# Attention output, norm and first feed-forward products of layer 2, rearranged by token block

## The chip, the cores and the metric

The kernel runs on one core of a Trainium2 chip. The metric is the device time of one execution in microseconds (us); the time before is the median of three runs. PE is the matrix engine (TensorE), PEld its weight loads, DVE the vector engine, ACT the scalar (activation) engine, POOL GpSimd, and SP the engine whose queue issues most weight loads.

## The reference

A trunk of two layers over 256 latent tokens and 256 context tokens of width 1024. Layer 1 mixes tokens with an mLSTM, layer 2 with multi-head latent attention; each is followed by a gated feed-forward with a short convolution over time. The change lies in layer 2, where only the latent tokens are still needed:

```python
x = _layer_norm(ALPHA * x + ml[2] * yl, ln_g[i, 0], ln_b[i, 0])      # yl = attention output @ w_out
f = _conv_ffn(_modulate(x, ml[3], ml[4]), ffn_w_in[i], ffn_conv_w[i], ffn_conv_b[i], ffn_w_out[i])
x = _layer_norm(ALPHA * x + ml[5] * f, ln_g[i, 1], ln_b[i, 1])

def _conv_ffn(h, w_in, conv_w, conv_b, w_out):
    gate, up = jnp.split(h @ w_in, 2, axis=-1)                       # FFN_DIM = 2816 columns each
    return (jax.nn.silu(_dwconv(gate, conv_w, conv_b)) * up) @ w_out
```

## The kernel before, in words

**Numbers in two parts.** Every product is made in a rounded format (`F32R`): an operand is split into a high part (a rounded copy, made by ACT) and a low part (the rest, `tensor_sub` on DVE). A product is then three matmuls: high by high, high by low, low by high (`mm3`, lines 395, 396 and 397).

**Weights.** `Stream` brings the weights in, in one fixed order, as tiles of 128 x 1024. `_load` issues the transfer on SP's queue into a raw tile; `_split` lets ACT make the high part (L334) and DVE the low part (L337), and then frees the raw tile. Around the change the raw tiles have nine places, reused in a ring, and a load is issued only when a place of its kind is free. Tiles marked wide (the last seven of `aout`, and of `fin1` those of p = 0 and 1) are split into two tiles `wu` of the pool `u` (31 tiles); the others into one of three tiles `w`. `use` hands over the next weight tile and splits ahead, up to eight tiles and up to `st.limit`; `pump(n)` splits up to tile n. In the order, the eight tiles `aout` come first, then the tiles `fin1` (p, j) for p = 0 to 21, j = 0 for the gate and 1 for the up projection, then `fout1`.

**The stage.** The 256 latent tokens are two blocks (t = 0, 1) of 128. `outmm` multiplies the attention output by `aout`; its last seven tiles are taken block by block. Block 0 has two column pieces of 512, block 1 has one of 512 and two of 256 (`acc4(True)`), so that less is left to do after the last. `ln_rows` then works through both blocks: gate times product, plus residual, `bn_stats` by piece, `bn_aggr`, square root on ACT (L1164), and normalization on DVE (L1187) and ACT (L1189). `ln_T4` transposes both blocks on PE (L1243, tiles `zT`, two column groups of both blocks to a PSUM bank), with five filler matmuls (`IDLE`, L1248) between the blocks, and makes from each of the eight transposed column groups k the feed-forward's input: scale and shift on ACT (L1255) or DVE (L1257), high part on ACT (L1258), low part on DVE (L1259), 256 tokens at a time, into the tiles `h1u`. `h1u` holds, for each k, 256 high columns and then 256 low ones.

**The feed-forward.** `ffn_in` runs over p and j; for p = 0 and 1 a product is 24 matmuls of 256 columns by `mm3`. From p = 2 on (L1374) the high weights multiply high and low activations in one matmul of 512 columns, the low weights the 256 high ones: 8 + 8 matmuls; the two halves are then added by a copy on ACT (L1378) and an addition on DVE (L1379), in a tile `fs`. The convolution, SiLU and gate follow for each p (`conv`, L674 to L681, L1385, L1393, L1394). `ln_x` applies the norm's gain and bias to the normalized rows (L1282, L1283) and stores them for the residual of the last step; it is advanced one step at each product (`tick`).

**What sets the order.** The program's instructions go through a scheduler which orders each engine's work by its own estimate of when operands are ready and by the order of the program. `keep_in_program_order` (`pin`) fixes an instruction behind the one traced before it on its engine; `issue_after(x)` puts what is traced in its block behind x on x's engine. On the chip each engine works its own list in order. [...]

Of the kernel before, what the change touches and what calls it, by code (L numbers as in the profile page):

```python
# [23 lines left out]
ALPHA = float((2 * DEPTH) ** 0.25)  # L24
# [7 lines left out]
CW = 1024  # L32

NB, NRAW, NU, NS = 3, 3, 31, 15

SUMS = 5

IDLE = 5

AHEAD = 8  # L40
QA, QB, QC = 2, 4, 6
PA, PB, PC = 0, 2, 4

VE = {1: (3, 0), 2: (3, 0), 3: (3, 0)}
# [209 lines left out]
class Stream:  # L254


    def __init__(self, k, ids, order, ws):
        self.k, self.ids, self.order, self.ws = k, ids, order, ws
        self.n = len(order)
        self.nl = self.ns = self.nu = 0  # L260
        self.live, self.kept = [], []
        self.limit = self.n
        self.raw, self.hl, self.tags = {}, {}, {}
        self.nsum = 0

        keys = [x[0] for x in order]
# [47 lines left out]
    def _split(self):  # L314
        k, j = self.k, self.ns
        key, wide = self.order[j]
        cols = self.ids[key][1]
        while self.nl <= j:
            self._load()
        self.nsum = max(self.nsum, j)  # L320
        while self.nsum < min(j + SUMS, self.n):
            while self.nl <= self.nsum:
                self._load()
            self._sum(self.nsum)
            self.nsum += 1
# [8 lines left out]
        k.nc.scalar.copy(h[:, :cols], src)  # L334
        if key[0] in ("vt2", "yt2"):
            k.nc.scalar.dma_start(k.t2d[key[0][0], key[1], key[2]][:, :cols], src)
        k.nc.vector.tensor_sub(l[:, :cols], src, h[:, :cols])  # L337
        self.hl[j] = (h, l)
        self.ns += 1
        while self._room():  # L340
            self._load()

    def use(self, key, hold=False):
        i = self.nu
# [21 lines left out]
class K:  # L366
# [863 lines left out]
                    yield  # L1230
            yield

    def ln_T4(self, zs, A, B, dst):


        nc, pin = self.nc, self.tc.keep_in_program_order
        w = self.st.hl[self.st.nu][0]
        pts = [self.ps("zT") for _ in range(4)]
        idle = self.ps("idle")
        for t in range(2):  # L1240
            for k in range(8):
                o = (k % 2) * 256 + t * 128
                i = nc.tensor.transpose(pts[k // 2][:, o:o + 128], zs[t][:, k * 128:(k + 1) * 128], self.ident)  # L1243
                if t and not k:
                    pin(i)
            if not t:
                for _ in range(IDLE):
                    pin(nc.tensor.matmul(idle, w[:, 0:128], w[:, 0:512], start=True, stop=True))  # L1248

        def one(k):  # L1250
            c = slice((k % 2) * 256, (k % 2 + 1) * 256)
            p, m = pts[k // 2][:, c], tmp[:, c]
            hi, lo = dst(k)
            if k // 2 % 2 == 0:
                nc.scalar.activation(m, p, AF.Identity, bias=B[:, k:k + 1], scale=A[:, k:k + 1])  # L1255
            else:
                nc.vector.tensor_scalar(m, p, A[:, k:k + 1], B[:, k:k + 1], op0=ALU.mult, op1=ALU.add)  # L1257
            i = nc.scalar.copy(hi, m)  # L1258
            nc.vector.tensor_sub(lo, m, hi)  # L1259
            return i.ins  # L1260

        tmp = self.s2("zm")
        first = one(0)
        for k in range(1, 8):
            if k % 2 == 0:
                tmp = self.s2("zm")
            with self.tc.issue_after(first):
                one(k)
            if k % 2:
                yield  # L1270

    def ln_x(self, ln, zs, dst):

# [73 lines left out]
    def ffn_in(self, l, hT, n, nt, pre=(), both=None):  # L1347

        nc, st = self.nc, self.st
        cw, cb = self.smc("fcw%d" % l), self.smc("fcb%d" % l)  # L1350
        key = "fin%d" % l
        acts = []
        pre = list(pre)
        for p in range(NF):
            pss = []
            for j in range(2):
                if pre:
                    w, ps = pre.pop(0)
                    self.ffn_half(ps, w, hT, 1)
                    if not pre:  # L1360
                        st.unhold()
                else:
                    w = st.use((key, p, j))
                    ps = self.ps("fin")
                    if both is None or p < 2:
                        for k in range(8):
                            c = slice(k * 128, (k + 1) * 128)
                            self.mm3(ps[:, :n], (w[0][:, c], w[1][:, c]), hT(k), k == 0, k == 7)
                    else:

                        mms = [(0, k) for k in range(7)] + [(1, k) for k in range(8)] + [(0, 7)]
                        for i, (x, k) in enumerate(mms):
                            c = slice(k * 128, (k + 1) * 128)
                            nc.tensor.matmul(ps[:, :n] if x else ps, w[x][:, c],  # L1374
                                             hT(k)[0] if x else both(k), start=i == 0, stop=i == 15)
                    if both is not None and p > 1:
                        t = self.s2("fs")
                        nc.scalar.copy(t[:, n:2 * n], ps[:, n:2 * n])  # L1378
                        nc.vector.tensor_tensor(t[:, :n], ps[:, :n], t[:, n:2 * n], op=ALU.add)  # L1379
                        ps = t  # L1380
# [474 lines left out]
def build(tc, off, a, out):  # L1855
    es = ExitStack()
    with es:
        k = K(tc, es, off, a)
        nc = k.nc
# [52 lines left out]
        def after0(pss, xr, gate, g, ln, l, c, dst, xdst):  # L1912
# [4 lines left out]
            yield from (k.ln_T4(zs, A, B, dst) if l else k.ln_T(zs, A, B, dst, g == 1))  # L1917
            if xdst is not None:
                k.late.append(k.ln_x(ln, zs, xdst))

# [38 lines left out]
        def norm1(g, zs, stats, first):  # L1959
# [6 lines left out]
            if g:  # L1966
# [24 lines left out]
        st.limit = fi + QA  # L1991
        k.outmm("aout", range(8 - TAIL["aout"], 8), o1, pl, 0, 8, 1, True)
        oT = None
        h1u = [k.u("h1") for _ in range(4)]
        h1 = lambda i: tuple(h1u[i // 2][:, i % 2, n * 256:(n + 1) * 256] for n in range(2))
        x3d = k.dr.tile([2, 128, D], F32, name="x3d")
        k.bg = [after0(pl, xr, gate, 1, 2, 1, 3, h1,
                       [x3d[0], x3d[1]])]
        k.tick(1)
        st.pump(fi + QB)  # L2000
        k.tick(1)
        st.pump(fi + QC)
        k.drain()
        st.limit = st.n
        k.take_late()
        acts = k.ffn_in(1, h1, 256, 1, both=lambda i: h1u[i // 2][:, i % 2])
        k.drain()
        h1 = h1u = None
        act1 = lambda i: (acts[i][:, 0], acts[i][:, 1])
# [27 lines left out]
```

## Time and profile before

| | |
|---|---|
| runs | 1359.81, 1359.42, 1362.17 us (median 1359.81) |
| the profiled execution | 1359.2 us; its span, first to last instruction, 1357.4 us |
| granted TensorE clock | 0.999 |
| PE busy | 1342.4 us, 99% of the span |
| DVE, ACT busy | 1056.4 us (78%), 711.9 us (52%) |
| attention output to feed-forward | about 1139 to 1176.5 us of the span |
| first products of layer 2's feed-forward (p = 0, 1) | 1164.9 to 1176.5 us |
| the later ones (p = 2 to 21) | 1176.5 to about 1288 us |

Times within the profile are counted from the start of the span. In a row of a timeline stand start, length, engine, line, operation, output and inputs, shapes, and in brackets the idle time before it with the instruction that ended it. A matmul's length is longer than its step: back-to-back matmuls overlap, and the distance of their starts is what they cost.

### The profile page before, as it was taken

The numbers are of one execution on the slowest core, as the hardware profiler recorded it, in microseconds if no ns is written. First come the engines' busy times: TensorE is split into PE (matmuls) and PEld (weight loads), VectorE is DVE, ScalarE is ACT, GpSimd is POOL, SyncE is SP. The second block draws the span as 40 slices with busy tenths as digits, with TensorE's granted clock in tenths as the row PEclk, the third lists the DMA queues.
The fourth block names the chain that finished last, engine by engine and source line by source line (L and its number), as shares of the span: only waits on it lengthen the run. The fifth ranks groups of instructions, "written<-read, shape, count | busy, mean of one in ns | idle before, by whom it ended". The sixth has DMA issues, their size and how long they took to land.

```text
span 1357.4 us, 18736 instructions
## 1 busy us (share of the span) xinstructions
PE 1342.4 (99%) x6663; PEld 1120.6 (83%) x6663; DVE 1056.4 (78%) x1731; ACT 711.9 (52%) x1236; POOL 122.1 (9%) x216
## 2 busy tenths in 40 slices
PE   9999999999999999999999999999999999999997
PEld 6777888888888888888898888888888888888886
DVE  4787756677688697897979878667898889888873
ACT  4764544445734545464644334334557767466660
POOL 0122000011101011030001000000001000000100
PEclk9999999999999999999999999999999999999999
DMA  9887848789676374785727877646997436366750
GB/s 368 315 271 269 294 162 245 235 289 304 215 250 194 98 246 142 239 297 190 232 92 250 295 234 236 213 148 215 309 279 220 140 102 223 104 192 188 256 194 31
DMA packets 92078, 297.73 MB, mean 219 GB/s; under 512 B 12073, under 2 KB 16425, under 8 KB 91985
## 3 DMA queue, kind: packets, MB, share of 16 engines
q1 hardware_dynamic: 62848, 218.65, 48.7%
q0 software_dynamic: 17472, 57.57, 13.6%
q10 hardware_dynamic: 11664, 20.32, 4.2%
q8 instruction: 52, 0.85, 0.3%
q14 instruction: 42, 0.34, 0.1%
HBM read 263.03 MB, written 33.46 MB: 218 GB/s over the span
## 4 chain that ended last, share of the span: by engine, by line
PE 93%; DMA 3%; DVE 2%; ACT 1%; issue 1%; ACTq 0%; SPq 0%; DVEq 0%
PE fin L1374 8%; PE y L396 6%; PE y L397 6%; PE y L395 6%; PE fin L395 6%; PE fin L396 6%; PE fin L397 6%; PE tok L395 6%; PE tok L396 6%; PE tok L397 6%; PE qk L395 4%; PE qk L397 4%; PE qk L396 4%; DMA adaw<-in_ada 2%; PE up L395 2%; PE up L397 1%
## 5 line engine op out<-in xcount | busy, mean ns | idle before, releaser
L337 DVE TENSOR_TENSOR w<-raw,w 128x1024 fp32r<-128x1024 f32 (+2 forms) x286 | 343.8, 1204 | 140.0 <-ACT w L334 139.2
L334 ACT CAST w<-raw 128x1024 fp32r<-128x1024 f32 (+2 forms) x286 | 297.2, 1039 | 290.8 <-PE tok L397 78.4
L500 DVE SCALAR_TENSOR_TENSOR junk<-ar,bc 128x1024 f32<-128x1024 f32 x128 | 156.2, 1220 | 4.0 <-ACT bc L542 1.4
L396 PE MATMUL fin<-h,w 128*128 128x512 f32 (+1 forms) x376 | 141.2, 376 | 0.0
L397 PE MATMUL fin<-h,w 128*128 128x512 f32 (+1 forms) x376 | 140.9, 375 | 0.0
L395 PE MATMUL fin<-h,w 128*128 128x512 f32 (+1 forms) x376 | 140.8, 376 | 0.1
L1374 PE MATMUL fin<-h,w 128*128 128x256 f32 (+1 forms) x640 | 111.9, 337 | 0.0
L1374 PEld LDWEIGHTS fin<-h,w 128*128 128x128 f32 x640 | 98.3, 190 | 13.4
L395 PE MATMUL qk<-xc,w 128*128 128x512 f32 x256 | 100.6, 393 | 0.0
L397 PE MATMUL qk<-xc,w 128*128 128x512 f32 x256 | 99.9, 390 | 0.0
L396 PE MATMUL qk<-xc,w 128*128 128x512 f32 x256 | 99.8, 390 | 0.0
L396 PEld LDWEIGHTS fin<-h,w 128*128 128x128 f32 x376 | 70.8, 188 | 12.9 <-DVE h L1228 0.2
L397 PEld LDWEIGHTS fin<-h,w 128*128 128x128 f32 x376 | 70.8, 188 | 12.9
L395 PEld LDWEIGHTS fin<-h,w 128*128 128x128 f32 x376 | 70.5, 188 | 13.1 <-ACT h L1227 0.3
L397 PEld LDWEIGHTS qk<-xc,w 128*128 128x128 f32 x256 | 48.1, 188 | 9.8
L396 PEld LDWEIGHTS qk<-xc,w 128*128 128x128 f32 x256 | 48.1, 188 | 9.7
L395 PEld LDWEIGHTS qk<-xc,w 128*128 128x128 f32 x256 | 48.1, 188 | 9.7
L395 PE MATMUL tok<-w,hT 128*128 128x512 f32 x128 | 49.9, 390 | 0.0
L397 PE MATMUL tok<-w,hT 128*128 128x512 f32 x128 | 49.8, 389 | 0.0
L396 PE MATMUL tok<-w,hT 128*128 128x512 f32 x128 | 49.8, 389 | 0.0
L681 ACT ACTIVATE fg<-fg 128x512 f32<-128x512 f32 (+1 forms) x44 | 23.2, 527 | 46.1 <-DVE fg L679 39.9
L337 DVE TENSOR_TENSOR wu<-raw,wu 128x1024 fp32r<-128x1024 f32 (+1 forms) x37 | 43.7, 1204 | 4.1 <-ACT wu L334 3.9
(470 smaller groups left out, 3142.3 us busy)
## 6 DMA issues: line engine op xcount, KB each, us to landing
raw<-in_ws SPq DMA_DIRECT2D x282, 512.0 KB, 4.6
ar<-in_adaT SPq DMA_DIRECT2D x80, 512.0 KB, 4.6
adaw<-in_ada SPq DMA_DIRECT2D x16, 512.0 KB, 8.0
t2d<-raw ACTq DMA_DIRECT2D x13, 512.0 KB, 4.8
raw<-t2d SPq DMA_DIRECT2D x13, 512.0 KB, 6.6
raw<-in_ws POOLq DMA_DIRECT2D x13, 512.0 KB, 7.9
zr<-fd ACTq DMA_DIRECT2D x33, 128.0 KB, 4.6
xmd<-xr POOLq DMA_DIRECT2D x16, 256.0 KB, 4.8
```

The costliest lines, as they stand in the source:

```text
L334: k.nc.scalar.copy(h[:, :cols], src)
L337: k.nc.vector.tensor_sub(l[:, :cols], src, h[:, :cols])
L395: mm(out, w[0], x[0], start=start, stop=False, skip_group_check=on)
L396: mm(out, w[0], x[1], start=False, stop=False, skip_group_check=on)
L397: mm(out, w[1], x[0], start=False, stop=stop, skip_group_check=on)
L500: nc.vector.scalar_tensor_tensor(o, w, 1.0, self.bc[j], op0=ALU.mult, op1=ALU.mult, accum_out=col[:, k, j:j + 1])
L681: nc.scalar.activation(tmp[:, :n], tmp[:, :n], AF.Silu)
L1374: nc.tensor.matmul(ps[:, :n] if x else ps, w[x][:, c], hT(k)[0] if x else both(k), start=i == 0, stop=i == 15)
```

## The change

`ln_T4` and the call of `after0` for layer 2 go; a new function `aout_fin` writes the stage out by token block.

- All `aout` tiles are split; then the four tiles `fin1` of p = 0 and 1 get their high parts only, and (2, 0) both. `Stream._split` leaves the low parts undone while `st.later` is a list; the raw tiles stay occupied until `low` is called.
- Block 0 is summed and normalized (on ACT alone) while PE multiplies block 1. Its eight transposes come between the second and the third column piece of block 1, into two banks.
- For block 0, column groups 0 to 5 are scaled, shifted and split before the sums of block 1's last piece on DVE, and groups 6 and 7 behind them. Each group is now done for one block, 128 tokens wide; for every other group ACT writes the high part straight from PSUM, and DVE repeats the scaling for the low part.
- The four first products take the high weights first: `high(0, ...)` multiplies block 0's high and low columns in one matmul of 256 columns (two runs of 128), six groups before block 1's transposes (`FILL`), two behind them; then `high(1, ...)` the same for block 1.
- Product (2, 0) follows whole (`both_mm`); then the low parts of the four weight tiles are made on DVE and their eight matmuls each follow.
- `ffn_in` now adds the two halves by the `fs` copy and addition for every p. The filler matmuls are gone.

```diff
@@ Stream._split
-        raw = self.raw.pop(j)
+        raw = self.raw[j]
         if wide:
-            h, l = [k.pool.tile([128, CW], F32R, tag="u", name="wu", bufs=NU) for _ in range(2)]
+            h, l = self.unit(), None
+            if self.later is None:
+                l = self.unit()
...
-        k.nc.vector.tensor_sub(l[:, :cols], src, h[:, :cols])
-        self.hl[j] = (h, l)
+        self.hl[j] = [h, l]
         self.ns += 1
+        if l is None:
+            self.later.append((j, src, self.hl[j]))
+        else:
+            self.low(j, src, h, l)
...
+    def low(self, j, src, h, l):
+        n = src.shape[1]
+        i = self.k.nc.vector.tensor_sub(l[:, :n], src, h[:, :n])
+        self.raw.pop(j)
+        return i
@@ K: ln_T4 is replaced by
+    def aout_fin(self, o1, pl, xr, gate, fi, h1u):
...
+        st.pump(fi)
+        st.later = []
+        st.pump(fi + 5)
+        low, st.later = st.later, None
...
+        def norm(t):
+            z, mv, rs, nm = zs[t], mvs[t], rss[t], nms[t]
+            pin(nc.vector.reciprocal(rs, rs))
+            pin(nc.vector.scalar_tensor_tensor(nm, mv[:, 0:1], -1.0, rs, op0=ALU.mult, op1=ALU.mult))
+            for a, b in ((0, 256), (256, 768)) if t else ():
+                pin(nc.vector.tensor_scalar(z[:, a:b], z[:, a:b], mv[:, 0:1], rs, op0=ALU.subtract, op1=ALU.mult))
+            for a, b in ((768, 1024),) if t else ((0, 512), (512, 1024)):
+                nc.scalar.activation(z[:, a:b], z[:, a:b], AF.Identity, bias=nm, scale=rs)
...
+        def cols(t, pts, ks, direct):
+            for k in ks:
...
+                if k in direct:
+                    nc.scalar.activation(hi, p, AF.Identity, bias=B[:, k:k + 1], scale=A[:, k:k + 1])
+                    pin(nc.vector.tensor_scalar(m, p, A[:, k:k + 1], B[:, k:k + 1], op0=ALU.mult, op1=ALU.add))
+                else:
+                    nc.scalar.activation(m, p, AF.Identity, bias=B[:, k:k + 1], scale=A[:, k:k + 1])
+                    nc.scalar.copy(hi, m)
+                pin(nc.vector.tensor_sub(lo, m, hi))
+
+        def part(ap, t):
+            return ap.rearrange("p (x t c) -> p t x c", x=2, t=2)[:, t]
+
+        def high(t, ks, fixed=False):
+            for k in ks:
+                for ps, w in zip(pss, wf):
+                    q = mm(part(ps, t), w[0][:, k * 128:(k + 1) * 128], part(h1u[k // 2][:, k % 2], t),
+                           start=k == 0, stop=False, skip_group_check=True)
...
+        rows(0, 0)
+        rows(0, 1)
+        sums(0, 0)
+        sums(0, 1)
+        root(0)
+        norm(0)
+        rows(1, 0)
+        sums(1, 0)
+        rows(1, 1)
+        sums(1, 1)
+        pts = turn(0)
+        cols(0, pts, range(6), (0, 2, 4))
+        rows(1, 2, True)
+        st.unhold("aout")
+        sums(1, 2)
+        root(1)
+        cols(0, pts, range(6, 8), ())
+        norm(1)
+        wf = [st.use(("fin1", p, j)) for p in range(2) for j in range(2)]
+        pss = [self.ps("fin") for _ in range(4)]
+        high(0, range(FILL))
+        pts = turn(1)
+        high(0, range(FILL, 8), True)
+        cols(1, pts, range(8), (0, 2, 4, 6))
+        high(1, range(8))
+        w2 = st.use(("fin1", 2, 0))
+        p2 = self.ps("fin")
+        self.both_mm(p2, w2, h1u)
+        fixed = True
+        for ps, w, (j, src, hl) in zip(pss, wf, low):
+            w[1] = st.unit()
+            i = pin(st.low(j, src, w[0], w[1]))
+            for k in range(8):
+                q = mm(ps[:, 0:256], w[1][:, k * 128:(k + 1) * 128], h1u[k // 2][:, k % 2, 0:256],
+                       start=False, stop=k == 7, skip_group_check=True)
...
+        with self.tc.issue_after(i.ins):
+            st.pump(fi + 7)
+        return pss + [p2]
@@ K.ffn_in, build
-                    if both is None or p < 2:
...
+                if both is not None:
+                    if pre:
+                        ps = pre.pop(0)
+                    else:
...
+                        self.both_mm(ps, w, both)
+                    t = self.s2("fs")
+                    nc.scalar.copy(t[:, n:2 * n], ps[:, n:2 * n])
+                    nc.vector.tensor_tensor(t[:, :n], ps[:, :n], t[:, n:2 * n], op=ALU.add)
...
-        k.outmm("aout", range(8 - TAIL["aout"], 8), o1, pl, 0, 8, 1, True)
+        pre = k.aout_fin(o1, pl, xr, gate, fi, h1u)
```

`rows(t, i)` are the matmuls of one column piece, `sums(t, i)` its gate, residual and `bn_stats` (three pinned DVE steps), `root(t)` the `bn_aggr` and the square root, and `turn(t)` the eight transposes, the first of them pinned.

More of the change, by code (lines that the diff above doesn't have):

```diff
@@ L36 @@
 SUMS = 5
-IDLE = 5
+FILL = 6
 AHEAD = 8
-QA, QB, QC = 2, 4, 6
 PA, PB, PC = 0, 2, 4
@@ L264, in __init__ @@
         self.nsum = 0
+        self.later = None
         keys = [x[0] for x in order]
@@ L1231, in ln_T @@
             yield
[L1233 to L1240, printed above, removed]
-            for k in range(8):
[L1242 to L1270, printed above, removed]
@@ L1272, in ln_x, with both_mm @@
+    def both_mm(self, ps, w, h1u):
+        mms = [(0, k) for k in range(7)] + [(1, k) for k in range(8)] + [(0, 7)]
+        for i, (x, k) in enumerate(mms):
+            h = h1u[k // 2][:, k % 2]
+            self.nc.tensor.matmul(ps[:, 0:256] if x else ps, w[x][:, k * 128:(k + 1) * 128],
+                                  h[:, 0:256] if x else h, start=i == 0, stop=i == 15)
     def ln_x(self, ln, zs, dst):
@@ L1356, in ffn_in @@
             for j in range(2):
-                if pre:
+                if both is not None:
+                    if pre:
+                        ps = pre.pop(0)
+                    else:
+                        w = st.use((key, p, j))
+                        ps = self.ps("fin")
+                        self.both_mm(ps, w, both)
+                    t = self.s2("fs")
+                    nc.scalar.copy(t[:, n:2 * n], ps[:, n:2 * n])
+                    nc.vector.tensor_tensor(t[:, :n], ps[:, :n], t[:, n:2 * n], op=ALU.add)
+                    ps = t
+                elif pre:
                     w, ps = pre.pop(0)
@@ L1364, in ffn_in @@
                     ps = self.ps("fin")
-                    if both is None or p < 2:
[L1366 to L1380, printed above, removed]
+                    for k in range(8):
+                        c = slice(k * 128, (k + 1) * 128)
+                        self.mm3(ps[:, :n], (w[0][:, c], w[1][:, c]), hT(k), k == 0, k == 7)
                 pss.append(ps)
@@ L1916, in after0 @@
             zs = k.zs
-            yield from (k.ln_T4(zs, A, B, dst) if l else k.ln_T(zs, A, B, dst, g == 1))
+            yield from k.ln_T(zs, A, B, dst, g == 1)
             if xdst is not None:
@@ L1990, in build @@
         fi = [x[0] for x in order].index(("fin1", 0, 0))
-        st.limit = fi + QA
-        k.outmm("aout", range(8 - TAIL["aout"], 8), o1, pl, 0, 8, 1, True)
+        st.limit = fi
+        h1u = [k.u("h1") for _ in range(4)]
+        x3d = k.dr.tile([2, 128, D], F32, name="x3d")
+        pre = k.aout_fin(o1, pl, xr, gate, fi, h1u)
         oT = None
[L1994 to L2003, printed above, removed]
+        k.late.append(k.ln_x(2, k.zs, [x3d[0], x3d[1]]))
         st.limit = st.n
         k.take_late()
-        acts = k.ffn_in(1, h1, 256, 1, both=lambda i: h1u[i // 2][:, i % 2])
+        acts = k.ffn_in(1, None, 256, 1, pre, both=h1u)
         k.drain()
```

49 lines of the change are left out of this document (added).

## The prediction

> **What bounds the kernel now.** I read the page first, then the chain that ended last, then the stage of the change engine by engine. The page's busy shares and the chain say who holds the end:
>
> ```profile
> span 1357.4 us, 18736 instructions
> PE 1342.4 (99%) x6663; PEld 1120.6 (83%) x6663; DVE 1056.4 (78%) x1731; ACT 711.9 (52%) x1236; POOL 122.1 (9%) x216
> PE 93%; DMA 3%; DVE 2%; ACT 1%; issue 1%; ACTq 0%; SPq 0%; DVEq 0%
> ```
>
> PE is the bound nearly everywhere, so only a stretch in which it does nothing useful can be won. The chain (start, length, what) shows one between the attention output (`y`) and the feed-forward (`fin`), and none in the 111.74 us behind it:
>
> ```profile
> 1160.65 0.44 DVE z L1157
> 1161.11 0.43 DVE z L1158
> 1161.57 0.44 DVE st L1160
> 1162.03 0.25 DVE mv L1162
> 1162.31 0.30 ACT rs L1164
> 1162.99 0.34 DVE z L1187
> 1163.37 0.45 PE zT L1243 x2
> 1163.85 0.57 ACT zm L1255
> 1164.44 0.41 ACT h L1258
> 1164.90 0.74 PE fin L395 x4
> 1176.67 111.74 PE fin L1374 x640
> ```
>
> The last column piece of `y` must be multiplied by the gate, added to the residual, measured, rooted, normalized, transposed, scaled and rounded before PE may go on. The timeline of PE in that stage (start, length, line, operation, idle before and its releaser):
>
> ```profile
> 1155.42 0.28 PE L395 MATMUL y<-wu,oT 128*128 128x256 f32 x1
> 1157.94 0.28 PE L395 MATMUL y<-wu,oT 128*128 128x256 f32 x1
> 1160.34 0.28 PE L397 MATMUL y<-wu,oT 128*128 128x256 f32 x1
> 1160.52 1.37 PE L1243 MATMUL zT<-ident,z 128*128 128x128 f32 x8
> 1161.64 1.40 PE L1248 MATMUL idle<-wu 128*128 128x512 f32 x5
> 1163.37 1.25 PE L1243 MATMUL zT<-ident,z 128*128 128x128 f32 x8 [0.33 <-DVE z L1187]
> 1176.50 15.74 PE L1374 MATMUL fin<-h,w 128*128 128x512 f32 x87
> ```
>
> Each of the last two pieces is 21 matmuls of 256 columns: 1155.42 to 1157.94, 0.12 us each; so `y` frees PE at 1160.34 + 0.12 = 1160.46. The next 16.04 us, to 1176.50, hold 96 useful `fin` matmuls (1164.90 to 1176.50: 11.60 us, 0.121 each) and 16 transposes (eight from 1160.52 to 1161.64 are 1.12 us, all 2.24). The rest, 16.04 - 11.60 - 2.24 = **2.20 us**, is waiting, the five filler matmuls among it. It is all that the stage can give: 0.16% of 1359.8.
>
> **The change part by part.** No product is saved: 32 + 32 high matmuls of 256 columns (two runs of 128, the high and the low activations of one token block) and 32 of low weights are again 96, and product (2, 0), moved ahead of the low ones, costs what each of the long row costs, 111.74 / 40 = 2.79 us. I follow the new order on PE with these durations.
>
> *Block 0.* Its eight transposes go between the second and the third column piece of block 1, 1157.94 to 1159.06, so the third piece ends at 1159.06 + 2.52 = 1161.58. They need block 0 normalized by 1157.94. Before, it was late, because DVE was full of weight splits:
>
> ```profile
> 1145.90 3.49 DVE L337 TENSOR_TENSOR wu<-raw,wu 128x1024 fp32r<-128x1024 f32 x3
> 1155.17 1.22 DVE L337 TENSOR_TENSOR wu<-raw,wu 128x1024 fp32r<-128x1024 f32 x1
> 1158.14 0.42 DVE L1157 TENSOR_TENSOR z<-y,gate 128x256 f32<-128x256 f32 x1 [0.35 <-PE y L397]
> 1159.65 1.52 ACT L1189 ACTIVATE z<-z,nm,rs 128x512 f32<-128x512 f32 x2 [2.81 <-DVE nm L1167]
> ```
>
> A split's subtraction takes 3.49 / 3, some 1.15 us. Four of them, those of the first four `fin1` tiles, leave this place; block 0's last `y` column is done near 1155.42 - 21 x 0.227 = 1150.65 (0.227 is 2.79 less eight times 0.121, by eight), and the tail of 1160.65 to 1163.37 at double width, with 1.52 us of ACT, ends by 1156. I cost this at nothing; its cover is 2 us.
>
> *The columns of block 0, pieces 0 to 5.* DVE first sums the second piece of block 1, from 1158.14 for three steps of 0.46 us (chain, 1160.65 to 1162.03), to 1159.52. Then come three scalings and six subtractions, 128 columns wide, which no row of this stage shows. The nearest, of the first layer's heads, and the 256-wide ones of this stage:
>
> ```profile
> 404.43 0.69 ACT L1023 ACTIVATE W<-Am,gcol 128x128 f32<-128x128 f32 x2
> 405.02 0.40 ACT L1023 ACTIVATE W<-aB,gcol 128x128 f32<-128x128 f32 x1
> 408.15 0.61 DVE L1041 SCALAR_TENSOR_TENSOR W<-W,R,W 128x128 f32<-128x128 f32 x2
> 1164.44 0.54 DVE L1257 TENSOR_SCALAR zm<-zT,lnA,lnB 128x256 f32<-128x256 f32 x1 [0.67 <-PE zT L1243]
> 1164.90 0.42 DVE L1259 TENSOR_TENSOR h<-zm,h 128x256 fp32r<-128x256 f32 x1
> ```
>
> ACT: two in 405.02 - 404.43 = 0.59, 0.30 each. DVE: two in 0.61, 0.30 each; upper end 0.46, the step of the 256-wide pair (1164.90 - 1164.44); a gain is excluded, since the halves replace one whole. I take 0.30, the row of the same width. Then DVE ends these columns at 1159.52 + 9 x 0.30 = 1162.2; ACT, with nine operations from about 1158.8, at 1161.5. PE's first 24 high matmuls run from 1161.58 to 1164.48 and find their pieces in time.
>
> *The added wait.* DVE's order is pinned, so the sums of the last piece stand behind those columns: they start at 1162.2, not 1161.8. Three steps of 0.46 end at 1163.6, and from there the chain above needs 1163.37 - 1162.03 = 1.34 to block 1's transposes: 1164.95. PE was free at 1164.48: a **new stall of 0.47 us**. PE's whole queue stands behind these transposes.
>
> [...]
>
> *Block 1.* Transposes to 1166.07; the remaining eight high matmuls (0.97) to 1167.04. The columns need four transposes of a bank (0.56) and some 0.3 of latency (1163.37 to 1163.85, less two transposes of 0.14): 1165.8. Both engines then need 12 operations x 0.30 = 3.6 us, 0.45 a piece; PE takes 4 x 0.121 = 0.48 a piece from 1167.04. They keep ahead by about half a microsecond, and the high matmuls end at 1170.91, product (2, 0) at 1173.70.
>
> *The low parts.* DVE turns to them at about 1169.7: ready at 1170.8, 1172.0, 1173.1, 1174.3. PE takes them from 1173.70 in steps of 0.97 to **1177.57**; the last would start at 1176.6. The cover is product (2, 0); without it the first would be just in time and the last 0.5 late. At nothing go the `fs` copies and additions of products 0 to 3, the splits queued behind the last low part, and the held loads, for these rows:
>
> ```profile
> L1378 ACT COPY fs<-fin 128x256 f32<-128x256 f32 x8 | 3.0, 374 | 7.7 <-PE fin L1374 7.7
> L1379 DVE TENSOR_TENSOR fs<-fin,fs 128x256 f32<-128x256 f32 x8 | 3.4, 422 | 3.0 <-ACT fs L1378 3.0
> 1169.10 1.29 DVE L1282 TENSOR_TENSOR z<-z,gr 128x512 f32<-128x512 f32 x2
> 1176.50:1190.00 13.50, 13.50 (x79) 11.86 (x78) 8.89 (x16) 7.95 (x15) 0.54 (x1) 1.00 0.36 108
> raw<-in_ws SPq DMA_DIRECT2D x15, 512.0 KB, 4.6
> ```
>
> Four of each make 1.5 us of ACT and 1.7 of DVE; in 1176.5 to 1190 (PE busy, PEld, DVE, ACT) DVE has 4.6 us free. The split of (2, 1) is ready near 1175.5; its low half is first used at 1177.57 + 7 x 0.227 = 1179.2. SP's queue: four raw tiles stay occupied until the low parts, so of nine places five hold the next tiles, and (4, 1) or so waits until about 1170.8; it lands 4.6 us later and is wanted four products on, near 1188.7.
>
> **The sum.** Before, the same work including (2, 0) ended at 1176.50 + 2.79 = 1179.29; now at 1177.57: 1.72 us, or 2.20 less 0.47. Nothing behind it gives it back, as the chain is PE's from there on. The profiled execution took 1359.2, its span 1357.4; 1359.2 - 1.7 = 1357.5, and the median of the runs shown, 1359.81, becomes **1358.1 us**. With 0.46 instead of 0.30, the columns of block 0 end 1.4 later, the stall is 1.9 and block 1's columns, 5.5 us, hold PE another microsecond or more: the gain falls to zero or just below.
>
> **The rivals.** Within 0.2% means within 2.7 us, about what a measurement of this kernel can tell from no change.
>
> *Faster: waits ahead of the stage go too.* PE and ACT wait a little in the attention's end:
>
> ```profile
> 1132.69 0.39 PE L396 MATMUL o<-PT,v 128*128 128x256 f32 x1 [0.37 <-DVE PT L401]
> 1139.82 0.35 PE L395 MATMUL o<-PT,v 128*128 128x256 f32 x1 [0.21 <-DVE oT L401]
> 1137.03 1.05 ACT L334 CAST w<-raw 128x1024 fp32r<-128x1024 f32 x1 [2.06 <-DMA raw<-in_ws]
> ```
>
> The four subtractions leave DVE and the order of the splits changes; if 0.37 and 0.21 went as well as all 2.20, the gain would be 2.8: 1357.0. For it: both waits end with DVE. Against: the splits that leave come mostly after 1143, and 2.20 asks for no stall at all.
>
> *Same: the cover fails.* The final scaling of block 0 (`ln_x`, eight steps of 0.61, 4.9 us) may slip into DVE's pinned chain wherever that waits for ACT, since nothing pins it. All before the last low part: ready at 1174.3 + 4.9 = 1179.2, end 1180.2, 0.9 slower than before: 1360.7. For it: its tile is free once block 0 is transposed. Against: before, it came only after the last column, at 1169.10.
>
> *Slower: the split operand.* The 64 high matmuls read and write two runs of 128, which no row shows. Lower end 0.121, as contiguous; upper end two transposes, 2 x 0.14 = 0.28: 64 x 0.16 = 10.2, which gives 1368.3. From 4.4 / 64 = 0.07 each the change is slower by over 2.7. For it: nothing in the rows. Against: the runs are long, and 256 and 512 columns cost nearly in proportion.
>
> *It doesn't overlap:* if no tile is free for block 0's columns until the `aout` weights are released, they start near 1161.7, the sums at 1164.7, the transposes at 1167.4: 2.45 later, 1360.5, which falls under same.
>
> **How the numbers follow.** Forecast 0.46, its own range 1357.6 to 1359.0; faster by the waits ahead 0.24; cover fails or no overlap 0.16; split operand 0.14. So faster by over 0.2% has 0.24, within 0.62, slower 0.14. The range 1356.5 to 1361.5 takes in the first three and leaves out the split operand and the tails.
>
> **What would show it.** Right: no `idle` at L1248's place, eight `zT` between two `y` pieces, under 0.6 us idle ahead of the second eight, `fin` without a gap from there. Wrong: idle ahead of low matmuls with releaser DVE `wu` (cover), high matmuls over 0.15 apart (split operand), `ln_x` steps between sums and transposes, or a `zT` that starts after the last `y`.

## The result, and the profile after

| | before | after |
|---|---|---|
| median (runs) | 1360.19 us (8, 1359.42 to 1362.17) | 1364.13 us (8, 1363.55 to 1365.82) |
| ratio to before, 95% interval | | 1.0031, 1.0022 to 1.0040 |
| the profiled execution | 1359.2 us, span 1357.4 | 1364.14 us, span 1362.4 |

The change makes the kernel slower by 0.3%, some 4 us, where 1.7 us less were forecast. The page of the changed kernel hides the loss: PE is still "99%" busy, DVE 78% as before, and ACT has 3 us more.

```profile
span 1362.4 us, 18756 instructions
PE 1344.0 (99%) x6658; PEld 1122.4 (82%) x6658; DVE 1058.5 (78%) x1746; ACT 715.1 (52%) x1253; POOL 121.7 (9%) x216
```

The end of the chain shows it. Before, one unbroken run of `fin` L1374, 111.74 us long, followed the stage; now waits on DVE and ACT stand among the products (start, length, what):

```profile
1184.90 1.05 issue
1185.95 1.28 ACT L695
...
1192.66 1.13 DVE w L353
...
1194.52 1.15 DVE w L353
1195.71 97.62 PE fin L1379 x562
```

The timeline of PE in the changed kernel (start, length, line, operation, and in brackets the idle time before it and what ended it):

```profile
1157.73 1.03 PE L1299 MATMUL zT<-ident,z 128*128 128x128 f32 x8
1158.53 2.76 PE L1270 MATMUL y<-wu,oT 128*128 128x256 f32 x21
1161.12 2.75 PE L1326 MATMUL fin<-h,wu 128*128 128x256 f32 x20
1164.15 0.74 PE L1326 MATMUL fin<-h,wu 128*128 128x256 f32 x4 [0.29 <-DVE h L1318]
1166.72 2.00 PE L1299 MATMUL zT<-ident,z 128*128 128x128 f32 x8 [1.83 <-DVE z L1292]
...
1178.72 4.00 PE L1364 MATMUL fin<-h,wu 128*128 128x256 f32 x32
1182.56 9.86 PE L1379 MATMUL fin<-h,w 128*128 128x512 f32 x50
1193.85 1.45 PE L1379 MATMUL fin<-h,w 128*128 128x256 f32 x9 [1.43 <-DVE w L353]
1195.71 19.65 PE L1379 MATMUL fin<-h,w 128*128 128x256 f32 x115 [0.41 <-DVE w L353]
```

Up to the third piece's end all goes as forecast or better: block 0's transposes lie between two `y` pieces (1157.73, eight starts in 0.80 us), and the first high matmul starts at 1161.12. Then come 1.83 us of idling ahead of block 1's transposes instead of 0.47, the low matmuls (L1364) end at 1182.56 instead of 1177.57, and behind them PE waits 1.43 + 0.41 = 1.84 us for low weight parts. In the kernel before the same work ended at 1179.29; 1182.56 - 1179.29 = 3.27, and with the 1.84 it is 5.1. The spans differ by 5.0.

Product (2, 0) does not follow whole, as the section on the change has it: the order of PE's list put its matmuls (L1379) between block 1's high ones, from 1171.08 on. They fill the time in which block 1's columns are late, so the row shows no idling there.

**Where the longer stage comes from.** DVE and ACT at the columns of block 0 (same columns):

```profile
1159.19 0.40 DVE L1314 TENSOR_SCALAR zm<-zT,lnA,lnB 128x128 f32<-128x128 f32 x1
1159.63 0.29 DVE L1318 TENSOR_TENSOR h<-zm,h 128x128 fp32r<-128x128 f32 x1
1160.65 0.29 DVE L1318 TENSOR_TENSOR h<-zm,h 128x128 fp32r<-128x128 f32 x1 [0.73 <-ACT h L1317]
1160.86 0.41 DVE L1314 TENSOR_SCALAR zm<-zT,lnA,lnB 128x128 f32<-128x128 f32 x1
...
1164.02 0.42 DVE L1279 TENSOR_TENSOR z<-y,gate 128x256 f32<-128x256 f32 x1
```
```profile
1159.63 0.46 ACT L1316 ACTIVATE zm<-zT,lnB,lnA 128x128 f32<-128x128 f32 x1 [0.74 <-DVE zm L1314]
...
1161.30 0.46 ACT L1316 ACTIVATE zm<-zT,lnB,lnA 128x128 f32<-128x128 f32 x1 [0.32 <-DVE zm L1314]
...
1162.78 0.81 ACT L1316 ACTIVATE zm<-zT,lnB,lnA 128x128 f32<-128x128 f32 x2 [0.69 <-DVE zm L1314]
```

ACT's scaling of an odd group (L1316) starts when DVE's scaling of the even group before it (L1314) has ended: both read the transposes, different columns of one PSUM bank. DVE's next subtraction then waits for ACT's cast. The engines take turns, and neither is ever full. So six groups last from 1159.19 to 1164.02, 4.8 us instead of 2.7, and the sums of the last piece (L1279) start at 1164.02 instead of 1162.2. For block 1 it is 1168.40 to 1175.0, 6.6 us instead of 3.6. The groups scaled by DVE are also read by ACT (L1313), in the same bank. The waits for the tile `zm` from 1157 to 1176, with total and count ("its engine sat idle before it until"):

```profile
  ACT h L1317: 4.8, 7
  DVE zm L1314: 3.8, 6
  ACT h L1313: 1.3, 1
```

**The clock.** The same stretch by windows (PE, PEld, DVE, ACT, POOL busy, then the granted clock):

```profile
1164.00:1166.00 2.00, 0.74 (x4) 0.53 (x4) 1.88 (x8) 0.92 (x3) 0.00 (x0) 1.00 0.00 0
1166.25:1172.50 6.25, 5.78 (x25) 5.42 (x26) 3.35 (x11) 3.40 (x9) 0.00 (x0) 0.50 0.00 0
1173.00:1176.00 3.00, 3.00 (x21) 2.73 (x21) 2.15 (x5) 1.00 (x4) 0.00 (x0) 1.00 0.00 0
```

During the idling the granted clock fell to 0.50, and stayed there for some 6.8 us (1166.05 to 1172.9); the kernel before kept 1.00 through its stage.

**Behind the stage.** The subtraction that PE waits for at 1193.85 stands in DVE's list behind the final scaling of block 0 and block 1 (`ln_x`, L1392 and L1393):

```profile
1182.43 0.69 DVE L1392 TENSOR_TENSOR z<-z,gr 128x512 f32<-128x512 f32 x1
...
1187.69 0.43 DVE L1493 TENSOR_TENSOR fg<-fg,fs 128x256 f32<-128x256 f32 x1 [1.32 <-ACT fg L695]
...
1191.63 0.69 DVE L1393 TENSOR_TENSOR z<-z,br 128x512 f32<-128x512 f32 x1
1192.23 0.42 DVE L1502 TENSOR_TENSOR act<-fg,act 128x256 fp32r<-128x256 f32 x1
1192.57 1.22 DVE L353 TENSOR_TENSOR w<-raw,w 128x1024 fp32r<-128x1024 f32 x1
```

In this profile DVE's list also stood still for 1.32 us, until ACT had done a SiLU (L695); ACT was late with it because of a cast of weights (L336 at 1184.88, 1.05 us) and a table load of 1.28 us (1185.95). That is not needed for the wait: when the same kernel was profiled again (experiment 10), DVE had no such idling and PE waited 1.78 us all the same.

Three suspects, then: the shared bank, the clock, and DVE's backlog. Which of them carries the 4 us is the question of the experiments.

### The profile page after: what moved, and what is told of

It is laid out like the page before. It is cut to its first block, busy times and chain, and to the rows that moved or that the text cites. A ratio compares the mean times of both kernels' runs of the same rounds, so it can differ in the third digit from the quotient of the medians.

```text
span 1362.4 us, 18756 instructions
## 1 busy us (share of the span) xinstructions
PE 1344.0 (99%) x6658; PEld 1122.4 (82%) x6658; DVE 1058.5 (78%) x1746; ACT 715.1 (52%) x1253; POOL 121.7 (9%) x216
## 4 chain that ended last, share of the span: by engine, by line
PE 92%; DMA 3%; DVE 2%; ACT 2%; issue 1%; ACTq 0%; SPq 0%; DVEq 0%
PE fin L1379 8%; PE y L410 6%; PE y L411 6%; PE fin L410 6%; PE tok L409 6%; PE fin L409 6%; PE y L409 6%; PE fin L411 6%; PE tok L410 6%; PE tok L411 6%; PE qk L409 4%; PE qk L411 4%; PE qk L410 4%; DMA adaw<-in_ada 2%; PE up L409 2%; PE up L410 1%
## 5 line engine op out<-in xcount | busy, mean ns | idle before, releaser
L336 ACT CAST w<-raw 128x1024 fp32r<-128x1024 f32 (+2 forms) x286 | 296.6, 1037 | 293.0 <-PE tok L411 78.9
L410 PE MATMUL fin<-h,w 128*128 128x512 f32 (+1 forms) x376 | 141.2, 376 | 0.0
L411 PE MATMUL fin<-h,w 128*128 128x512 f32 (+1 forms) x376 | 140.9, 375 | 0.0
L409 PE MATMUL fin<-h,w 128*128 128x512 f32 (+1 forms) x376 | 140.8, 376 | 0.1
L1379 PE MATMUL fin<-h,w 128*128 128x512 f32 (+1 forms) x640 | 114.1, 338 | 1.8 <-DVE w L353 1.8
L1379 PEld LDWEIGHTS fin<-h,w 128*128 128x128 f32 x640 | 98.4, 190 | 15.4 <-DVE w L353 2.6
L695 ACT ACTIVATE fg<-fg 128x512 f32<-128x512 f32 (+1 forms) x44 | 23.1, 526 | 44.7 <-DVE fg L693 38.7
```

What stands on the lines that cost most here:

```text
L409: mm(out, w[0], x[0], start=start, stop=False, skip_group_check=on)
L410: mm(out, w[0], x[1], start=False, stop=False, skip_group_check=on)
L411: mm(out, w[1], x[0], start=False, stop=stop, skip_group_check=on)
L695: nc.scalar.activation(tmp[:, :n], tmp[:, :n], AF.Silu)
L1379: self.nc.tensor.matmul(ps[:, 0:256] if x else ps, w[x][:, k * 128:(k + 1) * 128], h[:, 0:256] if x else h, start=i == 0, stop=i == 15)
```

## The experiments

All but the fourth start from the changed kernel. Each set ran beside the kernel before, whose median was 1360.09 us (first four), 1360.39 (next four) and 1360.52 (last three).

**1. The banks.** Even column groups into one bank, odd ones into the other, so that ACT's odd groups and DVE's even ones never meet:

```diff
-            for k in range(8):
-                q = nc.tensor.transpose(pts[k // 4][:, k % 4 * 128:k % 4 * 128 + 128],
+            for k in (0, 2, 4, 6, 1, 3, 5, 7):
+                q = nc.tensor.transpose(pts[k % 2][:, k // 2 * 128:k // 2 * 128 + 128],
...
-                p, m = pts[k // 4][:, c], tmp[t][:, c]
+                p, m = pts[k % 2][:, k // 2 * 128:k // 2 * 128 + 128], tmp[t][:, c]
```

> The changed kernel with one thing altered: the eight transposed column groups of a block lie in the two PSUM banks by even and odd k instead of by halves, so that ACT's scaling of an odd group and DVE's of an even one touch different banks. Theory 'one bank at a time' (in the changed kernel ACT waits for DVE's scaling before each odd group, 3.8 us in six waits): DVE's stretch from its first to its last step on groups 0 to 5 of block 0 falls from 4.8 us to about 3.5, that of block 1 from 6.8 to about 4.5, PE's 1.8 us wait ahead of block 1's transposes falls below 1, the granted clock stays at 1.00, and the time is 3 to 5 us below the changed kernel's, near 1360. Rival 'narrow operations are simply dear, or the shared SBUF tile zm is what orders them': both stretches stay and so does the time, 1364.

Measured: 1360.51 us (12 runs), ratio 0.9999 (0.9990 to 1.0007). No operation was added or taken away, and both engines still share the tiles `zm` and `h1u`, yet 3.6 us are gone. The edit also alters the order of the transposes, and with it that of ACT's list. DVE's stretch over six groups of block 0 fell from 4.8 us to 3.1 (1161.16 to 1164.25), that over block 1 from 6.6 to 4.3 (1168.50 to 1172.78). The waits for `zm` in the same window, all that is left of the three lines above:

```profile
  ACT h L1313: 1.7, 3
```

Nobody waits for L1314 or L1317 any more; the wait that is left is in the bank of the even groups, which both engines still read. What PE did:

```profile
1163.08 3.04 PE L1326 MATMUL fin<-h,wu 128*128 128x256 f32 x24
1166.97 1.33 PE L1299 MATMUL zT<-ident,z 128*128 128x128 f32 x8 [0.85 <-DVE z L1292]
...
1179.89 3.43 PE L1379 MATMUL fin<-h,w 128*128 128x512 f32 x18
...
1192.23 23.14 PE L1379 MATMUL fin<-h,w 128*128 128x256 f32 x134 [0.41 <-DVE w L353]
```

From the first high matmul to the end of the low ones it takes 16.81 us, in the change 21.44 (19.20 at full clock, experiment 10). The wait behind also shrank, from 1.84 to 0.41, and the clock stayed at 1.00.

**2. Fillers for the clock.** Eight filler matmuls ahead of block 1's transposes:

```diff
         high(0, range(FILL))
+        idle = self.ps("idle")
+        for _ in range(8):
+            pin(mm(idle, wf[0][0][:, 0:128], wf[0][0][:, 0:512], start=True, stop=True))
         pts = turn(1)
```

> The changed kernel with eight filler matmuls of 512 columns put back between the 24th high matmul and block 1's transposes (8 x 0.227 = 1.8 us, the length of PE's wait there). Theory 'the fillers held the clock' (in the changed kernel the granted clock is 0.50 from about 1166.2 to 1172.7 us, which costs some 3 us of PE work): the clock stays at 1.00 through the stage, the transposes take 1.1 us instead of 1.65, and the time falls by 2 to 3 us, near 1361.5, since DVE's columns of block 1 then end the stage. Rival 'the columns on DVE and ACT end the stage anyhow, the slow clock is hidden': clock 1.00, time within 1 us of the changed kernel's, 1364.

Measured: 1364.41 us (7 runs), ratio 1.0029 (1.0019 to 1.0039): nothing won. In the profiled execution, the fastest of the seven, the clock was kept, and the stage was held by the columns:

```profile
1165.48 2.00 PE L1354 MATMUL idle<-wu 128*128 128x512 f32 x8
1167.48 1.33 PE L1299 MATMUL zT<-ident,z 128*128 128x128 f32 x8
...
1192.73 1.44 PE L1382 MATMUL fin<-h,w 128*128 128x256 f32 x9 [1.80 <-DVE w L353]
1194.60 20.57 PE L1382 MATMUL fin<-h,w 128*128 128x256 f32 x119 [0.42 <-DVE w L353]
```

The transposes start as late after the third piece as before (1167.48 - 1161.88 = 5.60; in the change 1166.72 - 1161.12 = 5.60), the stage takes 19.20 us, and the waits behind are 2.22.

In this profile PE is through with the waits 32.72 us after the first high matmul (1194.60 - 1161.88), in the change after 34.59 (1195.71 - 1161.12): an estimate of 1.9 us for what the slow clock cost in that one execution. The median does not show such a gain, but does not test it well either. The mean granted clock of the seven runs is 0.9973, as in experiment 10 (0.9974) and below the 0.9984 of the kernel before, so in most of them the clock probably fell somewhere in spite of the fillers.

**3. The background work later.** `take_late` releases the work put off until then, `ln_x` among it; it is called at p = 6 of the feed-forward instead of ahead of it:

```diff
-        k.take_late()
         acts = k.ffn_in(1, None
...
         for p in range(NF):
             pss = []
+            if both is not None and p == 6:
+                self.take_late()
```

> The changed kernel with the eight DVE steps of block scaling for the residual (ln_x) started only at p = 6 of the feed-forward. Theory 'DVE's backlog': the subtraction for weight tile (3, 1) stands in DVE's list behind them; without them PE's two waits for DVE's w (1.4 and 0.4 us near 1192.4 and 1195.3) go, and the time falls by 1.5 to 2 us, near 1362.3. Rival 'the waits move to a later tile, since DVE has the same work to do': time as the changed kernel's, 1364.

Measured: 1361.32 us (11 runs), ratio 1.0006 (0.9997 to 1.0014): 2.8 us back, and no wait of PE for `w` is left. This with the stage nearly as slow as in the change (20.41 us) and the clock at half for one stretch:

```profile
1168.85:1172.20 3.35, 3.35 (x16) 3.16 (x15) 1.98 (x7) 2.18 (x6) 0.00 (x0) 0.50 0.00 0
```

**4. The kernel before, without its fillers** (`IDLE = 0` instead of 5).

> The kernel before with its five filler matmuls left out and nothing else. It has 4.4 us without any matmul but 16 transposes, more than the 3.7 us after which the changed kernel's clock had fallen. Theory 'the fillers held the clock': the granted clock falls to 0.50 for some 6 us from the stage on, and the time rises by 2 to 3.5 us, to about 1363. Rival 'transposes keep the clock, and the changed kernel's clock fell for another reason': clock 1.00, time as before, 1360.2.

Measured: 1360.93 us (12 runs), ratio 1.0003 (0.9995 to 1.0012). Its profiled execution was the slowest of the twelve (1363.53 us). There the clock did fall, with a hole of 1.49 us ahead of the second transposes:

```profile
1163.00:1167.70 4.70, 2.91 (x20) 1.92 (x19) 3.05 (x9) 2.90 (x7) 0.00 (x0) 1.00 0.02 8
1167.75:1171.00 3.25, 3.25 (x15) 3.25 (x16) 3.19 (x10) 3.24 (x10) 0.00 (x0) 0.50 0.00 0
```

The stage took 1180.83 - 1163.29 = 17.5 us instead of 16.04, but the medians differ by 0.8, within the interval. So in the kernel before the fillers are not worth 4 us.

**5. Banks and late work together.**

> Both edits that helped by themselves: the column groups laid by even and odd number in the two banks, and the later start of the deferred background work. If the two losses are separate (bank turns in the stage; DVE's backlog behind it), the wait for DVE w that was left with the banks alone (0.41 us) is gone too, and the time is 0.3 to 0.6 us below the banks alone: 1360.0, within 0.1% of the kernel before. If the later start only helped because the stage ended late, the time stays at 1360.5 or rises, and DVE w waits show somewhere else in the long row.

Measured: 1359.08 us (11 runs), ratio 0.9994 (0.9985 to 1.0003); no wait for `w` in the long row. The later start is worth 2.8 us by itself and 1.4 on top of the banks, where the profile had only 0.41 us of waits left; the 1.4 is not clear of the two intervals. The wait of 1.84 us that shrank to 0.41 with the banks alone says that part of the backlog came from the late end of the columns.

**6. ACT alone.** The banks as in the change, but ACT scales every group, so DVE never reads a bank that ACT reads:

```diff
-        cols(0, pts, range(6), (0, 2, 4))
+        cols(0, pts, range(6), ())
...
-        cols(1, pts, range(8), (0, 2, 4, 6))
+        cols(1, pts, range(8), ())
```

> The changed kernel with ACT alone scaling all column groups (DVE only subtracts), banks as in the change. Bank theory: no other engine reads the banks, so ACT needs about 0.65 us a group (0.46 + 0.30 with overlap) without waiting: six groups 3.9 us, eight groups 5.2 us against 4.8 and 6.8 in the change; the sums of the last piece start about 1 us earlier, and the time is 2 to 3 us below the change: 1361 to 1362. Rival, that DVE's order or the number of narrow operations sets the pace and not the bank: with one operation more on ACT and one less on DVE per pair the stage is no shorter, 1364 or more.

Measured: 1359.98 us (11 runs), ratio 0.9998 (0.9990 to 1.0007), better than either theory had it. ACT does two groups in 1.09 us without a pause:

```profile
1159.35 0.81 ACT L1316 ACTIVATE zm<-zT,lnB,lnA 128x128 f32<-128x128 f32 x2 [2.98 <-PE zT L1299]
1160.05 0.49 ACT L1317 CAST h<-zm 128x128 fp32r<-128x128 f32 x2
1160.44 0.81 ACT L1316 ACTIVATE zm<-zT,lnB,lnA 128x128 f32<-128x128 f32 x2
```

One engine, with more operations than it had, is faster than two in turns: from ACT's first scaling of block 1 until DVE is free for the weights it takes 4.7 us (1166.63 to 1171.35), in the change 7.1 (1167.91 to 1174.96), with the banks apart 4.8 (1168.01 to 1172.78). Experiment 1 kept the operations and changed the banks; this one kept the banks and the order of the transposes and took away the second reader. Together they show that two readers of one bank made the turns.

**7 and 11. Late work with eight and with two fillers**, the edits of 2 (with the count 8 or 2) and 3 together.

> The later start with eight filler matmuls before the second transposes. In the later start alone the granted clock stood at 0.50 for about 3.4 us, with PE busy: a loss of 1.7 us. If that loss is real and the fillers (about 2.0 us, in a hole of 1.83) prevent it, the stage ends 1.2 to 1.6 us sooner, there is no wait for DVE w to give it back, and the time is 1359.8 to 1360.2. If the stage is set by the columns and not by PE's clock, as the equal times of fillers and change let one think, it stays at 1361.3.

> The later start with two filler matmuls (0.45 us) instead of none (1361.3, clock 0.50 for 3.4 us) or eight (1360.45, clock 1.00). About 1.3 us of the hole stay idle, ahead of 1.1 us of transposes. If so small a fill keeps the clock, 1360.0 to 1360.5; if the idle time must be filled nearly whole, 1361.3 with 0.50 in the windows after the transposes.

Measured: eight 1360.45 us (11 runs), ratio 1.0002 (0.9993 to 1.0011); two 1361.32 (11 runs), 1.0007 (0.9998 to 1.0016). In both profiles the clock stayed at 1.00 and the stage took 19.21 and 19.20 us. Against none (1361.32) eight may be worth 0.9 us, but the intervals overlap: inconclusive. The expectation that the half clock decides the median was wrong for two fillers.

**8. As 5, with block 0's groups 4 and 5 scaled by ACT** (`(0, 2)` for `(0, 2, 4)` in block 0's first call).

> As banks and later start together, and in block 0 ACT alone scales groups 4 and 5, so DVE has one scaling (0.41 us) less ahead of the sums of the last piece. With the banks apart a wait of 0.85 us ahead of block 1's transposes was left, released by DVE's normalization. If DVE's columns hold that wait, it shrinks to 0.4 to 0.5 and the time falls by 0.4 us against banks and later start; if ACT's extra cast holds the subtraction instead, nothing is won.

Measured: 1359.65 us (11 runs), ratio 0.9996 (0.9987 to 1.0004); the wait ahead of block 1's transposes is 0.79 instead of 0.85. Nothing won: the second case.

**9. ACT alone, and late work.**

> ACT alone scales the columns, and the deferred background work starts later. With ACT alone the stage ended 0.35 us sooner than with the banks apart (at equal ends of y), and 0.56 us of waits for DVE w were left behind it; without them the time is 1358.5 to 1359.3, at or just below banks and later start together (1359.1). If DVE's backlog is made by the columns on DVE and not by the background work, the waits stay and the time is 1360.0.

Measured: **1358.57 us** (11 runs, 1357.66 to 1359.62), ratio 0.9986 (0.9977 to 0.9995): faster than both kernels. PE:

```profile
1162.18 3.04 PE L1326 MATMUL fin<-h,wu 128*128 128x256 f32 x24
1165.76 1.33 PE L1299 MATMUL zT<-ident,z 128*128 128x128 f32 x8 [0.54 <-DVE z L1292]
1166.85 2.44 PE L1326 MATMUL fin<-h,wu 128*128 128x256 f32 x16
...
1174.82 4.00 PE L1364 MATMUL fin<-h,wu 128*128 128x256 f32 x32
1178.66 36.72 PE L1379 MATMUL fin<-h,w 128*128 128x512 f32 x209
```

One wait is left, 0.54 us, where the forecast had 0.47, and no wait for `w` behind it. With the banks apart and the later start (5) the median was 1359.08; the two are not clearly apart.

**10. The change once more.**

> The changed kernel once more, beside these others. 1364 if the loss is as large here as before. Whether the half clock lasts two stretches of 3.4 us again, or one, is open: if it hangs on where a fixed window falls over the hole, it may differ from the first profile.

Measured: 1364.17 us (7 runs), ratio 1.0029 (1.0018 to 1.0040). The loss is the same, and so is the hole ahead of the transposes, 1.83 us, but the clock kept 1.00 there. It fell behind the second hole, where PE waited for `w`, for one stretch of 3.4 us:

```profile
1192.04 23.24 PE L1379 MATMUL fin<-h,w 128*128 128x256 f32 x127 [1.78 <-DVE w L353]
```
```profile
1162.00:1192.50 30.50, 26.55 (x171) 23.33 (x171) 25.66 (x56) 16.66 (x39) 2.17 (x4) 1.00 0.37 131
1193.00:1196.00 3.00, 3.00 (x13) 2.53 (x13) 3.00 (x6) 2.02 (x4) 0.00 (x0) 0.50 0.87 218
```

The runs side by side; stage, waits and clock are those of the profiled execution, the median is that of all runs. "Stage" is from the first high matmul (L1326) to the end of the low ones; for the kernel before the same work takes 16.04 + 2.79 less the eight transposes that now lie ahead of it (1.12), 17.71.

| kernel | stage, us | waits for `w` behind | clock at 0.50 for about | median, us |
|---|---|---|---|---|
| forecast | 15.99 | 0 | 0 | 1358.1 |
| before | 17.71 | 0 | 0 | 1360.1 to 1360.5 |
| change | 21.44 | 1.84 | 6.8 us, in the stage | 1364.13 |
| change again (10) | 19.20 | 1.78 | 3.4 us, behind it | 1364.17 |
| fillers (2) | 19.20 | 2.22 | 0 | 1364.41 |
| late (3) | 20.41 | 0 | 3.4 us, in the stage | 1361.32 |
| late, fillers 8 / 2 (7, 11) | 19.21 / 19.20 | 0 | 0 | 1360.45 / 1361.32 |
| banks (1) | 16.81 | 0.41 | 0 | 1360.51 |
| banks, late (5) / and 8 | 16.83 / 16.77 | 0 | 0 | 1359.08 / 1359.65 |
| ACT alone (6) | 16.49 | 0.56 | 0 | 1359.98 |
| ACT alone, late (9) | 16.48 | 0 | 0 | 1358.57 |

At full clock the stage has three lengths to within 0.1 us: 19.20 with the turns, 16.8 with the banks apart, 16.5 with ACT alone. Stage and waits together, against the row of the kernel before, give the medians to within 1.7 us; the change's own row, with the longest stretch of slow clock, is the farthest off. One profile of each can hardly do better, since the stage itself began at times between 1161.12 and 1163.08 from one profile to the next.

## Why the prediction was wrong

**What held.** Several costs came out as priced. The transposes fitted between the `y` pieces (1157.73 for a forecast 1157.94; third piece done at 1161.12 for 1161.58), so block 0 was normalized in time. High matmuls with two runs of 128 cost 0.12 us each (24 in 1162.18 to about 1165.1, experiment 9): the split operand, the rival with the large price, is nothing. The low parts were covered by (2, 0): L1364's 32 matmuls run without a gap in every trace. And `ln_x` did not slip into the pinned chain between sums and transposes.

**The step that failed first: ACT and DVE working on the columns at the same time.** The columns were costed as nine operations of 0.30 us on each engine for block 0 and twelve for block 1, both engines going at once. The price of an operation was fair. Where nothing is in the way (experiments 5 and 6) DVE's scaling and two subtractions take 1.0 us (1160.18 to 1161.19) and ACT's four operations 1.09, against 0.9 and 1.2 by the 0.30. What was wrong is that both go at once: the change put four groups into a bank and dealt them to the engines in turn. The code before had kept each bank to one engine (`if k // 2 % 2 == 0`, L1254, with two groups to a bank), and the diff showed the new split in two lines. It was read as a matter of balance. Block 0's six groups took 4.8 us for 2.7, block 1's eight 6.6 for 3.6, and the stall was 1.83 for 0.47. The price is 19.20 - 16.8 = 2.4 us of stage at full clock, of which 1.83 - 0.85 = 1.0 is the longer idling, and by the medians 3.6 with what follows from it, the shorter wait behind and the kept clock (experiment 1).

The prediction's upper end, 0.46 us an operation, gave a stall of 1.9. That 1.83 was measured is luck: the operations were not dearer, they waited. Its 0.3 us of latency ahead of block 1's columns is a slip, too (0.48 less two transposes of 0.14 is 0.20), but nothing hangs on it.

The waits show it: in the trace of the change ACT waited 3.8 us, in six waits, for DVE's L1314, and with the banks apart not at all for it. The prediction has no row of two engines reading one bank; the trace of the change is the first that measures it, and experiments 1 and 6 bear it out.

**The step that failed second: the work behind the low parts "at nothing".** The sum took DVE's 4.6 free microseconds in 1176.5 to 1190 as cover for the `fs` steps and the splits. But the four subtractions (4.62 us) began at 1174.96 behind the late columns, where 1169.7 was forecast, and used that room up. `ln_x`, 4.9 us, which the kernel before had done by 1175.7, now began at 1182.43 and stood ahead of the split that PE needed; the prediction names it as a danger for the stage only. PE waited 1.84 us; put off to p = 6 the waits are gone and 2.8 us are back (experiment 3), perhaps 1.4 where the columns are quick (5).

**What was left out: the clock.** The removed fillers were costed at nothing, without a word on the granted clock. It did fall in three profiles of the changed code (change, 3, 10), each time near a hole of 1.8 us, and is estimated at 1.9 us in the one execution of the change. How large it is in the median stays open: the runs of 2 were probably not free of it, taking the fillers from the kernel before cost 0.8 us within the interval (4), and eight of them beside the later start may be worth 0.9 (7). In the changed kernel it is not a cause apart from the other two. The holes near which it fell were made by the turns and the backlog, and with the banks apart, where the hole is 0.85 us, the mean clock of the runs is 0.9987.

With both failed steps mended (experiment 9) the forecast's own sum comes back: a stall of 0.54 for 0.47, a stage of 16.48 for 15.99, and a median 1.95 us below the kernel before, where 1.72 was forecast. That the median comes so close is in part luck: the two stages alone, 17.71 and 16.48, give 1.23.

## What to carry to other kernels

When work on a PSUM tile is dealt to two engines, deal it by bank, and cost it as taking turns where both read one bank: here six groups took 4.8 us in turns and 3.1 with the banks apart. A wait by turns shows as each engine's idle time ended by the other, with neither full (in the change, from 1157 to 1176, DVE waited 4.8 us for ACT's casts and ACT 3.8 for DVE's scalings). When subtractions are put off, look through the whole list of the engine that gets them, background work included, to the next instruction that PE needs, and not only to the end of the stage: here PE waited 1.84 us behind the stage. And before halves of a job are given to two engines, work out one engine alone: here it was as quick as two engines with the banks apart (a stage of 16.5 us against 16.8).

## What the hardware showed that I had not expected

In the windows of 0.25 and 0.5 us read, the granted clock stood at 1.00 or at 0.50, save in those in which it changed, and at 0.50 each time for about 3.4 us or twice that: 1168.9 to 1172.3 (late), 1167.7 to 1171.1 (before without fillers), 1192.8 to 1196.2 (change again), 1166.05 to 1172.9 (change). By the means of the windows in which it changed, the first three stretches last 3.42, 3.42 and 3.41 us, the last 6.83. A hole of 1.83 us brought it down in one profile of the change and not in the other, so what decides is not the hole alone.

In the 3.41 us before each fall PE was busy, transposes included, for 1.96 us (change), 1.56 (late), 1.65 (before without fillers) and 1.63 (change again). A low share does not decide alone either: over the first hole of the change again, from 1164.0 to 1167.5, PE was busy for 1.42 us of 3.5, and the clock stayed at 1.00.

Nor did the fall come at one place of a hole. In the change it came 1.2 us after the last product before the hole had ended (1164.89 to 1166.05), in the change again 0.8 us after products had begun once more behind it (1192.04 to 1192.8). What decides, a fixed window as the expectation of experiment 10 supposes or something else, was not shown, and no run was made to test it.
